# A hybrid trunk's layer: weights' sums in DRAM made later, rows' sums made in place block by block, and loads moved to GpSimd's queue

## The chip, the cores and the metric

The kernel runs on one core of a Trainium2 chip. The metric is device time in microseconds: the median of three executions. The trace is of one further execution, taken by the hardware profiler.

## The reference

One layer of a streaming encoder, float32, 1024 tokens (T) of width 1024 (D), and 256 memory tokens:

```python
h = layer_norm(a * x + stick_breaking(x @ sb_win) @ mix_wo)      # 16 heads of 64
h = layer_norm(a * h + cross_attention(h, mem) )                 # 4 heads of 256, with xa_wq, xa_wkv, xa_wo
u = h @ ffn_up                                                   # 1024 x 5632
u = causal_depthwise_conv(u, ffn_conv, width 3) + ffn_conv_b
g, val = split(u, 2)                                             # 2816 columns each
h = layer_norm(a * h + (gelu(g) * val) @ ffn_down)               # 2816 x 1024
```

with a = 2 ** 0.25; LayerNorm has a gain and a bias per column.

## The kernel before

**Products.** A float32 operand is split in two float32r parts, hi (a cast) and lo (the rest): `split` (lines 77 to 87). A product of two such operands is three matmuls, hi hi, hi lo, lo hi: `mm3` (lines 100 to 103). By default ScalarE casts (line 79) and VectorE subtracts (line 85); in some places GpSimd subtracts (line 87) or casts (line 83).

**Order.** The kernel is written in the program's order for a tile framework that assigns all semaphores. A planner with a simulated timeline then orders each engine's instructions: what is ready earlier in its simulation may go ahead of what is written earlier. An instruction in `keep_in_program_order` is not put ahead of the instruction written before it on its engine; others may pass it. Each engine, and each queue of DMAs (SyncE's, ScalarE's, GpSimd's), then works in that fixed order: a DMA that waits for a buffer holds those behind it. A tile of a pool with `reuse_waits="tile"` waits for the last use of just those older tiles whose memory it takes; `bufs` is the number of buffers that a tile name rotates through.

**Stages.** (1) Attention with all its projections; beside its end the memory's keys and values are made, and `wo` is split. (2) A loop of eight row blocks (`out_ln`, line 465): output projection (48 matmuls), residual, LayerNorm, transposes of the new rows. (3) Memory attention. (4) The same loop with the second LayerNorm; its rows go, transposed, into `h2f` (8 x 128 columns by 1024 rows) by `h2_evac`. (5) The MLP's first product (up), its convolution, GELU and gate, written to DRAM as `g_d`, 22 tiles of 128 x 1024. (6) The MLP's second product (down), the third LayerNorm, and the output.

**Both MLP products use seven products instead of eight on a 2 x 2 blocking (Strassen-Winograd).** They need sums of blocks of both factors.

*Up.* The rows' sums are t1 = b12 - b11, t2 = b22 - t1, t4 = b21 - t2 and t3 = b22 - b12, with b the four blocks of `h2f`. t3 is made in `h2_evac` per row block (line 596). The other three are made behind the loop, for k = 0 to 3, 12 subtractions of 128 x 512 (lines 707 to 713), each followed by its split. They take their memory from the three buffers `wt`, which are those of the weights' sums s1 to s4 (`Pair.sum`, line 630). The up weights come in 22 pairs of 128 columns; `Pair.block` (line 613) loads two blocks of 512 KB a pair (`wraw`, `wr`, two buffers each). Of the first two pairs the early products (`early1`, inside the last row block, and `early2`) run before the rows' sums are there, and `late` the rest. Then each step of the loop at line 792 runs `stage2` of a pair, `stage1` of the next, `stage3` of the pair. A pair ends in `gated`: convolution on ScalarE and VectorE, and for the second pair of two the gate product (line 739) and the store to `g_d` (line 740; on GpSimd's queue for the last pair).

*Down.* The weights' sums u1 to u4 are made in DRAM by DMAs alone (`u_steps`, line 419): 44 copies of 256 KB on SyncE's queue, then 44 DMAs on GpSimd's queue that add another block to what is there. They are interleaved in the two `out_ln` loops, six after the work of a block in the first loop, six ahead of a block in the second, as long as there are any. The down product runs seven products named m = 1, 6, 5, 7, 4, 3 and the last ("2", from line 945), each of 11 steps kt with four row blocks of 12 matmuls in all. A step loads a quarter of a gated tile (`slot(kt, s)`, 256 KB, line 824), a block of weights or of their sum (`w_block`, line 832, through pairs of `wraw`), splits both, and multiplies. Gated quarters are combined in place on VectorE (`plus`, line 854): in m = 1 slot 1 becomes slot 1 - slot 3 in the same step kt (line 905). The residual rows of h2 are loaded by `residual` (line 847) into two buffers `h2r` and added to an output quarter. In m = 4 a second weight block, "21", is loaded and split for the last product (line 917). The slots for kt under 5 are in the pool `ea`, the others in `ep`, behind the eight output rows `y`; both pools take memory that the MLP's first half had.

*End.* `finish` does the third LayerNorm of 128 rows and stores them. With `spread` it is shared: scale and bias on ScalarE, times the gain on GpSimd, plus the bias on VectorE, for each half of 512 columns (lines 452 to 456).

## Time and profile before

| | |
|---|---|
| time, median of 3 (lowest to highest) | 1591.94 us (1590.37 to 1593.48) |
| profiled execution: its time, its span | 1592.65 us, 1590.9 us |
| TensorE | 1521.3 us busy, 7508 matmuls |
| VectorE | 1100.6 us busy |
| ScalarE | 703.9 us busy |
| GpSimd | 643.4 us busy |
| mean granted TensorE clock | 0.981 of full speed |

The span goes from the first to the last instruction. PE is TensorE's matmuls, DVE VectorE, ACT ScalarE, POOL GpSimd, SPq SyncE's queue of DMAs; L85 is line 85. Matmuls overlap, so that a full stretch shows PE busy all the time, and the number of matmuls in it is the better measure. The granted clock is given in parts of 2.4 GHz; there are two levels, 1.00 and 0.50, so a value between them is a mean of both.

### The profile page before, as it was taken

How to read it: one execution, taken by the hardware profiler on the slowest of the kernel's cores; microseconds unless marked ns; L12 is line 12 of the kernel's file. 1: busy time of each engine (PE TensorE's matmuls, PEld its weight loads, DVE VectorE, ACT ScalarE, POOL GpSimd, SP SyncE). 2: the span in 40 equal slices, each digit the busy share in tenths (PEclk: the TensorE clock that was granted, in tenths of full speed). 3: DMA queues.
4: the chain of work that ended last, by engine and by line, in shares of the span. 5: the costliest groups of instructions: out<-in, count | busy, mean ns of one | idle time of the engine just before them, and what ended most of it. 6: DMA issues, size and time to landing. Idle time of an engine off the chain costs nothing.

```text
span 1590.9 us, 20977 instructions
## 1 busy us (share of the span) xinstructions
PE 1521.3 (96%) x7508; PEld 1267.0 (80%) x7508; DVE 1100.6 (69%) x1502; ACT 703.9 (44%) x1310; POOL 643.4 (40%) x571
## 2 busy tenths in 40 slices
PE   7999999999988999999999979999999999899897
PEld 5888888888877988788877757888888888688775
DVE  3366667667679646465445899877777777868795
ACT  4454555565566511133323244444444444344451
POOL 5775565565568800366405542323322231000033
PEclk9999999999999999999999989999999999899998
DMA  5322222221236548734449912222222224834531
GB/s 169 87 53 64 63 57 67 64 70 54 64 118 196 186 157 274 225 112 124 103 140 254 222 56 93 80 80 80 80 81 80 83 89 153 308 109 153 167 130 60
DMA packets 99192, 191.00 MB, mean 120 GB/s; under 512 B 11408, under 2 KB 33040, under 8 KB 99088
## 3 DMA queue, kind: packets, MB, share of 16 engines
q1 hardware_dynamic: 84400, 159.25, 31.5%
q0 software_dynamic: 6624, 12.59, 4.5%
q10 hardware_dynamic: 8064, 17.83, 3.2%
q8 instruction: 59, 0.97, 0.3%
q14 instruction: 45, 0.37, 0.1%
HBM read 146.63 MB, written 57.67 MB: 128 GB/s over the span
## 4 chain that ended last, share of the span: by engine, by line
PE 72%; DVE 10%; DMA 8%; POOL 4%; issue 4%; ACT 2%; SPq 1%; DVEq 0%; ACTq 0%; POOLq 0%
PE qkacc L101 4%; PE qkacc L103 3%; PE qkacc L102 3%; PE tp L231 3%; PE mb L101 3%; PE mb L103 3%; PE mb L102 3%; PE y L102 3%; PE y L103 3%; PE y L101 3%; PE ma L103 2%; PE ma L101 2%; PE ma L102 2%; PE mc L101 2%; PE mc L102 2%
## 5 line engine op out<-in xcount | busy, mean ns | idle before, releaser
L222 DVE TENSOR_TENSOR_SCAN sig<-sig 128x896 f32<-128x896 f32 (+7 forms) x128 | 196.8, 1544 | 73.9 <-POOL sig L219 55.2
L87 POOL TENSOR_TENSOR whl<-wraw,whl 128x512 fp32r<-128x512 f32 (+2 forms) x97 | 173.9, 1804 | 144.4 <-ACT whl L79 142.8
L448 POOL TENSOR_TENSOR rs<-rs,mhalf 128x1 f32<-128x1 f32 x24 | 23.7, 989 | 326.2 <-DVE rs L447 326.2
L85 DVE TENSOR_TENSOR wT<-tp,wT 128x512 fp32r<-128x512 f32 (+1 forms) x160 | 98.8, 629 | 62.4 <-ACT wT L79 61.2
L79 ACT CAST wT<-tp 128x512 fp32r<-128x512 f32 (+1 forms) x160 | 86.5, 545 | 103.9 <-PE tp L231 98.2
L79 ACT CAST whl<-wraw 128x512 fp32r<-128x512 f32 (+3 forms) x113 | 81.9, 738 | 97.6 <-PE y L103 34.5
L217 ACT ACTIVATE sig<-z 128x384 f32<-128x384 f32 (+2 forms) x192 | 92.1, 495 | 49.8 <-PE z L216 48.8
L101 PE MATMUL mb<-b_t,ws 128*128 128x512 f32 x264 | 105.0, 399 | 8.4 <-ACT ws L79 8.1
L101 PE MATMUL qkacc<-xh,whl 128*128 128x512 f32 x256 | 103.8, 405 | 7.6 <-ACT xh L79 6.2
L219 POOL TENSOR_SCALAR_AFFINE_SELECT sig<-sig 128x128 f32<-128x128 f32 x128 | 60.0, 472 | 119.5 <-ACT sig L217 113.6
L102 PE MATMUL y<-whl,aop 128*128 128x512 f32 x264 | 104.4, 397 | 1.6 <-DVE whl L85 1.6
L103 PE MATMUL mb<-b_t,ws 128*128 128x512 f32 x264 | 104.1, 396 | 0.0
L102 PE MATMUL mb<-b_t,ws 128*128 128x512 f32 x264 | 104.0, 394 | 0.0
L103 PE MATMUL qkacc<-xh,whl 128*128 128x512 f32 x256 | 101.9, 399 | 1.9 <-POOL whl L87 1.9
L102 PE MATMUL yacc<-wo,whl 128*128 128x512 f32 x256 | 102.4, 400 | 0.0
L102 PE MATMUL qkacc<-xl,whl 128*128 128x512 f32 x256 | 102.2, 399 | 0.0
L101 PE MATMUL yacc<-wo,whl 128*128 128x512 f32 x256 | 101.9, 398 | 0.2 <-ACT whl L79 0.2
L103 PE MATMUL y<-whl,aop 128*128 128x512 f32 x264 | 101.4, 396 | 0.0
L103 PE MATMUL yacc<-wo,whl 128*128 128x512 f32 x256 | 100.9, 396 | 0.0
L101 PE MATMUL y<-whl,aop 128*128 128x512 f32 x264 | 85.5, 398 | 12.3 <-ACT aop L79 7.6
L231 PE MATMUL tp<-ident,sig 128*128 128x128 f32 x576 | 89.4, 275 | 7.5 <-DVE wT L85 7.5
L79 ACT CAST ws<-wt 128x512 fp32r<-128x512 f32 x88 | 54.3, 620 | 95.5 <-PE mb L103 51.3
(214 smaller groups left out, 4355.6 us busy)
## 6 DMA issues: line engine op xcount, KB each, us to landing
u_d<-in_dn SPq DMA_DIRECT2D x44, 256.0 KB, 5.0
wraw<-in_up SPq DMA_DIRECT2D x22, 512.0 KB, 3.7
wr<-in_up SPq DMA_DIRECT2D x22, 512.0 KB, 3.6
float<-g_d SPq DMA_DIRECT2D x44, 256.0 KB, 5.6
wraw<-u_d SPq DMA_DIRECT2D x44, 256.0 KB, 2.9
g_d<-gate SPq DMA_DIRECT2D x20, 512.0 KB, 2.7
wraw<-in_dn SPq DMA_DIRECT2D x33, 256.0 KB, 3.0
q<-q SPq DMA_DIRECT2D x64, 128.0 KB, 2.2
```

The lines of the kernel that those rows point to most:

```text
L79: nc.scalar.copy(out=hi, in_=src)
L85: nc.vector.tensor_tensor(out=lo, in0=src, in1=hi.bitcast(F32), op=ALU.subtract)
L87: nc.gpsimd.tensor_tensor(out=lo, in0=src, in1=hi.bitcast(F32), op=ALU.subtract)
L101: nc.tensor.matmul(o, lhsT=lh, rhs=rh, start=first, stop=False, skip_group_check=more)
L102: nc.tensor.matmul(o, lhsT=lh, rhs=rl, start=False, stop=False, skip_group_check=more)
L103: nc.tensor.matmul(o, lhsT=ll, rhs=rh, start=False, stop=last, skip_group_check=more)
L217: nc.scalar.activation(out=sig[:, a:b], in_=z[:, :b - a], func=AF.Sigmoid, scale=-0.125)
L219: nc.gpsimd.affine_select(out=sig[:, S - P:S], in_=sig[:, S - P:S], pattern=[[-1, P]], base=-1, channel_multiplier=1, compare_op=ALU.is_ge ...
L222: nc.vector.tensor_tensor_scan(out=kr, data0=kr, data1=kr, initial=1.0, op0=ALU.mult, op1=ALU.bypass)
L231: nc.tensor.transpose(out=tp[:, k], in_=sigs[2 * d + u][:, P * j:P * j + P], identity=ident)
L448: nc.gpsimd.tensor_tensor(out=rs, in0=rs, in1=mhalf, op=ALU.pow)
```

## The change

- The generator of `u_steps` is made after the up product's first two pairs, and each step of the up loop takes five DMAs from it, ahead of `stage2`; both `out_ln` loops have none.
- t1, t2 and t4 are made in `h2_evac`, per row block of the second half, in `h2f` itself; behind the loop they are only split, t2 first.
- Gated quarters and the residual rows are loaded by GpSimd's queue; the residual rows have four buffers in `ep` instead of two in `ea`.
- In the down product the difference of m = 1 is made four steps later, the last four in m = 6; the weight block "21" of m = 4 has three buffers of its own.
- The LayerNorm of the very last row block is made without GpSimd's multiply: its first half by two operations on VectorE, its second by ScalarE and VectorE.

```diff
@@ -449,6 +449,15 @@
         if spread:
             nm = smallp.tile([P, 1], F32, name="nm")
             nc.vector.scalar_tensor_tensor(out=nm, in0=mv[:, 0:1], scalar=-1.0, in1=rs, op0=ALU.mult, op1=ALU.mult)
+            if spread == "last":
+                nc.scalar.activation(out=r[1], in_=r[1], func=AF.Identity, scale=rs, bias=nm)
+                nc.vector.scalar_tensor_tensor(out=r[0], in0=r[0], scalar=mv[:, 0:1], in1=g[:, 0:512],
+                                               op0=ALU.subtract, op1=ALU.mult)
+                nc.vector.scalar_tensor_tensor(out=r[0], in0=r[0], scalar=rs, in1=b[:, 0:512],
+                                               op0=ALU.mult, op1=ALU.add)
+                nc.vector.tensor_tensor(out=r[1], in0=r[1], in1=g[:, 512:], op=ALU.mult)
+                nc.vector.tensor_tensor(out=r[1], in0=r[1], in1=b[:, 512:], op=ALU.add)
+                return
             for c in range(2):
                 cs = slice(512 * c, 512 * c + 512)
                 nc.scalar.activation(out=r[c], in_=r[c], func=AF.Identity, scale=rs, bias=nm)
@@ -502,14 +511,11 @@
     def h1_evac(i, c, tp):
         split(tp, h1h[:, 4 * c:4 * c + 4, P * i:P * i + P], h1l[:, 4 * c:4 * c + 4, P * i:P * i + P])
 
-    u_sums = u_steps()
     with ExitStack() as c1:
         lnp = c1.enter_context(pool(name="ln1", bufs=1, side="right", reuse_waits="tile"))
         gb = load_ln(lnp, 0)
         for k, i in enumerate((4, 5, 2, 3, 0, 1, 6, 7)):
             out_ln(k, i, o_d, wts, xn, state["rp"], gb, h1_d, h1_evac)
-            for _ in range(6):
-                next(u_sums, None)
     mem_c.close()
 
 
@@ -593,9 +599,12 @@
         if th == 1 and c == 1:
             d = bs["t3"]
             t = lnp.tile([P, 4, P], F32, name="bt", bufs=2)
-            (nc.vector if i >= NTB - 2 else nc.gpsimd).tensor_tensor(
-                out=t, in0=h2f[:, 4:8, ts], in1=h2f[:, 0:4, ts], op=ALU.subtract)
+            b11, b21, b12, b22 = h2f[:, 0:4, cs], h2f[:, 4:8, cs], h2f[:, 0:4, ts], h2f[:, 4:8, ts]
+            (nc.vector if i >= NTB - 2 else nc.gpsimd).tensor_tensor(out=t, in0=b22, in1=b12, op=ALU.subtract)
             split(t, d[:, 0, :, cs], d[:, 1, :, cs])
+
+            for o, x, y in ((b11, b12, b11), (b12, b22, b11), (b21, b21, b12)):
+                nc.vector.tensor_tensor(out=o, in0=x, in1=y, op=ALU.subtract)
 
     e1c = ExitStack()
     e1 = {}
@@ -695,8 +704,6 @@
         rp = c3.enter_context(pool(name="rp2", bufs=2, reuse_waits="tile"))
         gb = load_ln(lnp, 1)
         for i in range(NTB):
-            for _ in range(6):
-                next(u_sums, None)
             out_ln(i, i, o2_d, wts2, h1_d, rp, gb, h2_d, h2_evac, first_products if i == NTB - 1 else None)
 
 
@@ -704,12 +711,9 @@
     bs.update({n: b3p.tile([P, 2, 4, 512], R, name=f"b_{n}") for n in ("t2", "t1", "t4")})
     for p in range(2):
         early2(pairs[p])
-    for k in range(4):
-        lo, hi = (slice(512 * th, 512 * th + 512) for th in range(2))
-        b11, b21, b12, b22 = h2f[:, k, lo], h2f[:, 4 + k, lo], h2f[:, k, hi], h2f[:, 4 + k, hi]
-        ts = [e1["a"].tile([P, 512], F32, name="wt", bufs=3) for _ in range(3)]
-        for t, n, x, y in ((ts[0], "t1", b12, b11), (ts[1], "t2", b22, ts[0]), (ts[2], "t4", b21, ts[1])):
-            nc.vector.tensor_tensor(out=t, in0=x, in1=y, op=ALU.subtract)
+    for n, k0, th in (("t2", 0, 1), ("t1", 0, 0), ("t4", 4, 0)):
+        for k in range(4):
+            t = h2f[:, k0 + k, 512 * th:512 * th + 512]
             split(t, bs[n][:, 0, k], bs[n][:, 1, k], "act", "pool" if n == "t4" else "dve")
     h2c.close()
     e1b = e1c.enter_context(pool(name="e1b", bufs=1, side="right", reuse_waits="tile"))
@@ -789,8 +793,11 @@
     late(pairs[1])
     pairs[2].factor("11", "s2", "s1")
     stage1(pairs[2])
+    u_sums = u_steps()
     for p in range(2, len(seq) - 1):
         w, nxt = pairs[p:p + 2]
+        for _ in range(5):
+            next(u_sums, None)
         stage2(w, nxt)
         if p + 1 < len(seq) - 1:
             nxt.factor("s2", "s1")
@@ -824,16 +831,19 @@
         def slot(kt, s):
             if (kt, s) not in slots:
                 t = slots[kt, s] = room(kt, s, F32)
-                nc.sync.dma_start(out=t, in_=g_d[NH * (s // 2) + kt][:, 512 * (s % 2):512 * (s % 2) + 512])
+                nc.gpsimd.dma_start(out=t, in_=g_d[NH * (s // 2) + kt][:, 512 * (s % 2):512 * (s % 2) + 512])
             return slots[kt, s]
 
         w_free = []
 
-        def w_block(n, kt):
-            if not w_free:
-                pair = wrawp.tile([P, 2, 512], F32, name="wraw")
-                w_free.extend((pair[:, 0], pair[:, 1]))
-            t = w_free.pop(0)
+        def w_block(n, kt, more=False):
+            if more:
+                t = ep.tile([P, 512], F32, name="wmore", bufs=3)
+            else:
+                if not w_free:
+                    pair = wrawp.tile([P, 2, 512], F32, name="wraw")
+                    w_free.extend((pair[:, 0], pair[:, 1]))
+                t = w_free.pop(0)
             nc.sync.dma_start(out=t, in_=u_d[n][kt] if n[0] == "u" else b_block(n, kt))
             return t
 
@@ -847,8 +857,8 @@
         def residual(n, b, x, op=ALU.add):
 
             i, ns = rows(n)[b]
-            t = ea.tile([P, 512], F32, name="h2r", bufs=2)
-            nc.sync.dma_start(out=t, in_=h2_d[i][:, ns])
+            t = ep.tile([P, 512], F32, name="h2r", bufs=4)
+            nc.gpsimd.dma_start(out=t, in_=h2_d[i][:, ns])
             nc.vector.scalar_tensor_tensor(out=quarters[n][b], in0=t, scalar=ALPHA, in1=x, op0=ALU.mult, op1=op)
 
         def plus(d, x, y, op=ALU.add):
@@ -895,14 +905,17 @@
                 s, u = plan[m]
                 x, t = slot(kt, s), ea.tile([P, 2, 512], R, name="aop", bufs=4)
                 if m == 6:
+                    if kt < 4:
+                        k7 = kt + NH - 4
+                        plus(slot(k7, 1), slot(k7, 1), slot(k7, 3), ALU.subtract)
                     plus(x, slot(kt, 1), x, ALU.subtract)
                 a, w = (t[:, 0], t[:, 1]), w_ops(kt)
                 split(x, *a)
                 split(w_block(u, kt), *w)
                 for b in range(4):
                     down(y[b], b, a, w, kt == 0 and not more, kt == NH - 1, more)
-                if m == 1:
-                    plus(slot(kt, 1), slot(kt, 1), slot(kt, 3), ALU.subtract)
+                if m == 1 and kt >= 4:
+                    plus(slot(kt - 4, 1), slot(kt - 4, 1), slot(kt - 4, 3), ALU.subtract)
                 elif m == 5:
                     nc.vector.scalar_tensor_tensor(out=slot(kt, 1), in0=slot(kt, 0), scalar=-1.0, in1=slot(kt, 3),
                                                    op0=ALU.mult, op1=ALU.subtract)
@@ -914,7 +927,7 @@
                         residual("11", kt - 7, c21[kt - 7])
                 elif m == 4:
                     last_ops[kt][1] = room(kt, 1, R), room(kt, 3, R)
-                    split(w_block("21", kt), *last_ops[kt][1])
+                    split(w_block("21", kt, True), *last_ops[kt][1])
                     if 3 <= kt < 7:
                         residual("21", kt - 3, c21[kt - 3])
                 elif m == 3:
@@ -948,7 +961,7 @@
                 down(y[b], b, *last_ops[kt], kt == 0, kt == NH - 1, False)
             plus(c11[b], c11[b], y[b])
             whole("11", b)
-            finish(b, True)
+            finish(b, "last" if b == 3 else True)
 
 
 def kernel(**inputs):
```

## Rows read from the trace of the kernel before

**Rows 1.** The page's busy time, share and instructions of each engine.
```profile
PE 1521.3 (96%) x7508; PEld 1267.0 (80%) x7508; DVE 1100.6 (69%) x1502; ACT 703.9 (44%) x1310; POOL 643.4 (40%) x571
```

**Rows 2.** Stretches: length, busy us (xinstructions) by engine, granted clock, DMA share, GB/s.
```profile
851.00:860.00 9.00, 6.75 (x27) 5.01 (x26) 8.25 (x16) 1.95 (x4) 5.95 (x7) 0.81 1.11 251
...
921.00:948.00 27.00, 17.61 (x67) 13.25 (x66) 24.58 (x37) 14.88 (x25) 8.07 (x6) 0.81 0.11 28
...
1000.00:1320.00 320.00, 320.00 (x1391) 260.77 (x1390) 242.86 (x282) 142.66 (x182) 94.33 (x52) 1.00 0.24 81
...
1364.00:1378.00 14.00, 6.58 (x18) 4.90 (x17) 7.46 (x9) 1.86 (x3) 0.84 (x2) 0.63 0.83 272
...
1378.00:1480.00 102.00, 102.00 (x452) 84.43 (x451) 79.96 (x129) 45.44 (x80) 0.00 (x0) 1.00 0.51 172
...
1480.00:1490.00 10.00, 5.26 (x16) 3.88 (x15) 8.07 (x15) 3.93 (x7) 0.00 (x0) 0.68 0.51 171
```

**Rows 3.** Timeline of PE: start, us, instructions, [idle before <-what ended it].
```profile
853.91 0.63 PE L493 MATMUL tp<-ident,r 128*128 128x128 f32 x4 [2.09 <-DVE r L462]
...
895.89 1.29 PE L493 MATMUL tp<-ident,r 128*128 128x128 f32 x8 [1.65 <-DVE r L462]
...
916.57 0.70 PE L493 MATMUL tp<-ident,r 128*128 128x128 f32 x4 [2.30 <-DVE r L462]
...
943.20 0.80 PE L101 MATMUL mb<-b_t,ws 128*128 128x512 f32 x1 [8.07 <-ACT ws L79]
...
1372.28 0.80 PE L101 MATMUL y<-whl,aop 128*128 128x512 f32 x1 [7.42 <-ACT aop L79]
...
1485.96 0.76 PE L101 MATMUL y<-whl,aop 128*128 128x512 f32 x1 [4.74 <-DVE y L855]
```

**Rows 4.** DMA issues in 840:900, 1000:1320 and 1466:1486: KB, median us to landing.
```profile
u_d<-u_d POOLq DMA_DIRECT2D x18, 256.0 KB, 12.4
...
r<-h_d ACTq DMA_DIRECT2D x10, 256.0 KB, 6.5
...
wr<-in_up SPq DMA_DIRECT2D x16, 512.0 KB, 3.5
...
g_d<-gate SPq DMA_DIRECT2D x16, 512.0 KB, 2.7
...
h2r<-h_d SPq DMA_DIRECT2D x7, 256.0 KB, 2.9
```

**Rows 5.** Timeline of POOL in the second LayerNorm loop.
```profile
887.22 5.04 POOL L426 DMA_DIRECT2D u_d<-u_d  x6
...
890.47 2.38 POOL L448 TENSOR_TENSOR rs<-rs,mhalf 128x1 f32<-128x1 f32 x1
```

**Rows 6.** DVE's groups by line in 900:950 and 1345:1364: busy, mean ns | idle.
```profile
L712 DVE TENSOR_TENSOR wt<-h2f,wt 128x512 f32<-128x512 f32 x8 | 6.9, 866 | 0.1
...
L855 DVE TENSOR_TENSOR float<-float,float 128x512 f32<-128x512 f32 x10 | 6.6, 683 | 0.0
```

**Rows 7.** Timeline of SPq and DVE in the up product.
```profile
1104.95 0.33 SPq L619 DMA_DIRECT2D wr<-in_up  x1
...
1116.29 0.69 DVE L631 TENSOR_TENSOR wt<-wr 128x512 f32<-128x512 f32 x1
```

**Rows 8.** Timeline of DVE, SPq and POOL at the turn to the down product.
```profile
1367.30 1.22 DVE L739 TENSOR_TENSOR gate<-gate,cv 128x1024 f32<-128x1024 f32 x1
...
1368.55 8.16 SPq L827 DMA_DIRECT2D float<-g_d  x13
...
1368.83 0.54 POOL L740 DMA_DIRECT2D g_d<-gate  x1 [4.53 <-DVE gate L739]
```

**Rows 9.** Timeline of SPq in the down product.
```profile
1472.93 4.99 SPq L851 DMA_DIRECT2D h2r<-h_d  x3
```

**Rows 10.** The chain that ended last, in order of time: start, us, what.
```profile
1582.07 0.56 POOL rs L448
...
1585.04 1.73 DVE y L456
```

## The prediction

> **What bounds the kernel now.** I read the page's busy times first: TensorE is busy 96% of the span and no other engine over 69% [rows 1]. So the time is TensorE's work plus the places where it waits, and the question is which of these places the change reaches. Next I read the stretches: the reader is to compare the number of matmuls with the length. In the MLP's steady products 1391 start in 320 us, 4.35 per us, at a granted clock of 1.00; in the down product 452 in 102 us, 4.43 per us. Against these paces three stretches fall short, and what is missing, divided by the pace, is the time lost there [rows 2]:
> - 921 to 948: 67 of 117 matmuls, 27 - 67/4.35 = 11.6 us.
> - 1364 to 1378: 18 of 62, 14 - 18/4.43 = 9.9 us.
> - 1480 to 1490: 16 of 44, 10 - 16/4.43 = 6.4 us.
>
> Part of each loss comes after the wait itself: the granted clock in these stretches is 0.81, 0.63 and 0.68 on average, so a part of each runs at the lower level, 1.2 GHz, after TensorE has stood. Last I read TensorE's own rows for who ended each wait: 8.07 us <- ScalarE's cast of a weights' sum, 7.42 us <- the cast of a gated block, 4.74 us <- VectorE, and in the second LayerNorm loop 2.09, 1.65 and 2.30 us <- VectorE's last LayerNorm step [rows 3].
>
> The profiled execution took 1592.65 us, 1.75 us more than its span and 0.71 us above the median of the three timed runs (1591.94). I sum against 1592.65 and take off 0.71 at the end.
>
> **Part 1, weights' sums out of the LayerNorm loops.** The 44 copies and 44 accumulating DMAs leave both loops. In 840 to 900 us 18 accumulating DMAs of one form run; they land after 12.4 us in the median, and a residual row of 256 KB beside them after 6.5 us, where a 256 KB row lands in 2.9 us late in the kernel [rows 4]. The wait at 853.91 follows such a late row: 2.09 us of standing and, in 851 to 860, a clock of 0.81, which is (1 - 0.81) x 9 = 1.7 us more [rows 2, 3]. Together 3.8, bounds 0 and 3.8; I take 2.8, since something can still be late by a little. The wait at 895.89 is GpSimd's: six accumulating issues hold it from 887.22 for 5.04 us, and the LayerNorm's power is stretched among them to 2.38 us (0.56 where nothing is near, at the end of the chain) [rows 5, 10]. That 1.65 us goes.
>
> Where they go: 5 per pair of up-product tiles, 18 iterations of 19.3 us each (7 products of 12 matmuls, 84/4.35). A weight block is loaded a pair ahead: issued at 1104.95, it lands 3.5 us later and VectorE first reads it at 1116.29, so it has 11.3 - 3.5 = 7.8 us to spare [rows 4, 7]. No trace shows the sums beside these loads. Nearest rows: a load beside the accumulating DMAs landed 3.6 us later than alone (6.5 against 2.9), inside the 7.8; the accumulating DMA itself took 12.4. GpSimd's issues, 5 x 0.84 = 4.2 us (5.04 for six), stand in front of GpSimd's next split; SP's five copies in front of the next weight load. Both are covered as long as less than 7.8 us is added. I take 1 us of loss in all; lower end 0 (nothing in this stretch is waiting now, so no gain), upper end 18 x (12.4 + 3.5 - 11.3) = 83 us, were every weight block as late as an accumulating DMA. I take the value near the first row because a plain load is what waits here, not an accumulation.
>
> **Part 2, sums of rows in place.** Before, 12 subtractions (L712, 0.87 us mean, some stretched) stand between the last row block and the first "late" product, interleaved with their splits, and the weights' sums of the first pair share their three buffers and queue behind them; that is the 8.07 us wait [rows 3, 6]. After, 9 of the 12 are done in earlier blocks, and 3 of 0.69 us remain behind the last one; the sums no longer share buffers. VectorE's work from the last transposes (921) to the first late product is then 3 pieces of t3 and b22 (2.1), 3 subtractions (2.1), 8 splits (5.5), sums and splits of the pair (3.4) and two combinations (1.3): 14.4 us, against 24 + 24 matmuls of early products, 11 us, and the first late product needs only the first half of it. So the wait goes save about 1.5 us: gain 10; bounds 4.8 (VectorE late by the whole 14.4 - 11 = 3.4, and as much again by the clock) and 11.6. The price: in the last four blocks VectorE gets 3 x 0.69 = 2.1 us more each, and in the last the wait of 2.30 us at 916.57 is already open [rows 3]. I charge 2.1 there, which eats the 1.65 of part 1; bounds 0 and 4 with the clock.
>
> **Part 3, gated rows by GpSimd's queue; deferred differences.** At the turn to the down product TensorE has the first five blocks' products and then waits for the sixth gated block. Its load is issued at 1368.55, right as the last gate product ends (1367.30 + 1.22) [rows 8]: its buffer lies on the convolution's scratch tile. That follows from the tile sizes too, counted in KiB of a partition from where these pools begin: 20 slots (40), operands (16), two h2r tiles (4) and lo2 (2) make 62, the eight output rows 32, so the slot lies at 94 to 96. From the other side, 182.6 less 38 for the weights' pool and 48 for the rows' sums leaves 96.6; the last 4 below it are the convolution's scratch, the 4 below those the second gate tile. With h2r's 4 gone from its pool the slot, still the first behind the output rows, lies at 90 to 92, on that gate tile, whose last reader is not VectorE but the store of it. So the load waits for the store to land: issue 0.54 [rows 8], landing 2.7 [rows 4], and its own issue on GpSimd is about 0.2 us longer than on SP (0.54 against 0.33, SP's of 1104.95 [rows 7]): 3.4 us later. (The Trainium skill, DMA: Bandwidth & Descriptors, Specifications, gives a first byte of about 1 us on GpSimd's path and 0.6 on SP's; no run here isolates that. By an estimate from this page the term is 0.4 us worse and the sum 0.4 lower.) Against it: 10 differences of 0.683 us stand in VectorE's queue in 1345 to 1364, among the last convolutions [rows 6]; the change defers five of them by four blocks. If half of them leave, the last gate ends 5 x 0.68 = 3.4 us earlier; I take 1.4, since the planner can put others there. Net loss 2; bounds -7 (nothing leaves, and the slow clock costs as much again as the 3.4) and +5 (all ten leave the last gate's way, 6.8, and the clock gains with it).
>
> **Part 4, residual rows on GpSimd's queue, weights of the second set in their own tiles.** The 4.74 us wait ends with VectorE's difference on the bank that the next product adds to. VectorE had stood behind residual rows, and ScalarE behind a weight block that SP issued late: three residual loads with two buffers hold SP from 1472.93 for 4.99 us, though one lands in 2.9 [rows 4, 9]. With the loads on another queue and four buffers SP only meets weights. Gain 5.5 of 6.4; bounds 0 and 6.4. (The Trainium skill, DMA: Bandwidth & Descriptors, Issuing engines are not separate DMA queues, says that issuing from several engines saves only the issue time, since all run on the same 16 DMA engines. By that rule nothing is gained here and the sum is 5.5 lower; it is a rival below. The trace speaks for the queue: it is held by waits for buffers, not by transfers.)
>
> **Part 5, last row block.** The chain's end: GpSimd's power at 1582.07 + 0.56, ScalarE, GpSimd's multiply, then VectorE's add from 1585.04, stretched to 1.73, and a second one of 0.6, to 1587.4 [rows 10]. After: four VectorE operations of 0.69 from the moment the scale and its product are there (1582.6 + 0.2), ending at 1585.6, with ScalarE beside the first two. Gain 1.8, bounds 1.5 (each 0.08 longer) and 2.4 (the first runs before the power).
>
> Sum: 2.8 + 1.65 - 2.1 + 10 - 2 + 5.5 + 1.8 - 1 = 16.65 us. 1592.65 - 16.65 = 1576.0; less 0.71: 1575.3 us.
>
> **Rivals.**
> - The turn gets shorter as well (part 3 at +5, parts 1, 2 and 4 at their full 3.8, 11.6, 6.4): 16.65 + 7 + 3.5 = 27.15 us, 1564.8. For it: VectorE is full in that stretch, and every difference gone counts. Against: the gate's store.
> - VectorE takes over from the wait at 943, as its 24.58 busy us in 27 say [rows 2]: part 2 gives 4.8 instead of 10, and the turn is at -7: 16.65 - 5.2 - 5 = 6.45, 1585.5. Against: 8 us of its work there are moved ahead.
> - A different queue saves only issue time: part 4 gives nothing, 11.15 us, 1580.8. For it: the moved bytes are the same, 0.51 of the DMA engines' time in 1480 to 1490 [rows 2]. Against: SP's row [rows 9]. This is also the way in which the change doesn't do what it says.
> - Slower: the sums in DRAM make weight blocks late. Place: VectorE's first sum of each pair, 18 times. It decides once a block lands more than 11.3 us after its issue; the whole gain is gone at 16.65/18 = 0.9 us more, 12.2 us, about an accumulating DMA's median [rows 4]. At 13 us: 18 x 1.7 = 30.6 us, against 17.65 of the other parts, 1604.9. For it: these DMAs fill the engines in 840 to 900. Against: there six came per row block of 11 us (48 matmuls at 4.4 per us) and here five per 19.3, and the DMA share of the up product is 0.24 now [rows 2].
>
> **Chances.** Forecast (gain 9 to 24) 0.55; shorter turn 0.13; VectorE takes over 0.12; issue time only 0.08; weight blocks late 0.09 (of it 0.02 within 0.2%); the rest 0.03, no change that shows. The measurement tells 0.2%, 3.2 us, from no change. Faster: 0.55 + 0.13 + 0.12 + 0.08 = 0.88; slower 0.07; same 0.05. Range: from 1563, past the shorter turn, to 1589, past VectorE's rival; about 0.2 lies outside. Forecast alone: 1568 to 1583.
>
> **What would show it.** In the profile after: no L426 rows before 1000; the LayerNorm power rows (L448) in the second loop near 1 us; no wait over 3 us and a clock of 1.00 between 920 and 950 (step 2); the wait at the turn 6 to 12 us, ended by a load issued after the gate's store landed (step 3); no wait of 4 us where the fourth product of the down part follows on the same banks (step 4); the last output issued 4 us after the last row's statistics (step 5). Wrong if TensorE's pace in the up product falls under 4.35 per us, or if the wait near 943 stays over 4 us.

## The result, and the profile after

The changed kernel takes 1571.19 us (median of four runs, 1568.83 to 1574.44) against 1591.15 us for the kernel before on the same chip (1585.77 to 1593.48): ratio 0.9881, 95% interval 0.9849 to 0.9912. Predicted were 1575.3 us, from 1563 to 1589. Its profiled execution took 1570.6 us with a span of 1568.8 us, so the spans differ by 22.1 us.

I place these 22.1 us first by the starts of a few matmuls that both kernels have, before looking at waits. The lengths of five stages, in us, and in the last column the gain that the prediction's terms give for the stage:

| stage | before | after | gain | predicted |
|---|---|---|---|---|
| start to the first output projection (code unchanged) | 561.3 | 559.2 | 2.1 | 0 |
| A: first LayerNorm loop and memory attention, to the last `o2acc` | 251.3 | 247.6 | 3.7 | 0 |
| B: second LayerNorm loop, to the last `yacc` | 92.6 | 83.2 | 9.4 | 2.8 + 1.65 |
| C: last row block and up product, to the last `mc` | 439.7 | 431.7 | 8.0 | 10 - 2.1 - 1 |
| D: down product, to the last `y` | 234.9 | 237.0 | -2.1 | 5.5 - 2 |
| E: from there to the end | 11.2 | 10.1 | 1.0 | 1.8 |

The first line is a measure of chance: nothing is changed there (and stage A came out 1.9 us shorter and 1.4 longer in two kernels below that are unchanged in it). So the sum came out near the forecast because two terms were too small by 8.7 us together (A, B) and one stage lost where it should have gained (D), 5.6 us the other way: that these two nearly cancel is luck.

The page's busy times after (answering to [rows 1]):

```profile
PE 1508.8 (96%) x7508; PEld 1261.5 (80%) x7508; DVE 1086.4 (69%) x1504; ACT 701.5 (45%) x1309; POOL 676.8 (43%) x629
```

Stretches of the changed kernel; the columns are those of [rows 2]. In order: the second LayerNorm loop, the last row block, the steady up product, the turn to the down product, the steady down product, and the place of the old wait ahead of the fourth product:

```profile
838.00:847.00 9.00, 9.00 (x45) 7.44 (x44) 8.46 (x16) 3.62 (x7) 0.99 (x1) 1.00 0.42 149
903.00:913.00 10.00, 5.68 (x17) 3.72 (x18) 8.81 (x16) 3.72 (x8) 2.92 (x1) 0.66 0.30 105
980.00:1300.00 320.00, 320.00 (x1391) 260.77 (x1390) 242.50 (x282) 143.42 (x182) 131.96 (x96) 1.00 0.53 140
1337.00:1364.00 27.00, 10.76 (x36) 8.32 (x35) 12.04 (x17) 5.53 (x9) 9.35 (x18) 0.68 0.67 234
1364.00:1466.00 102.00, 102.00 (x452) 84.42 (x451) 81.64 (x132) 45.39 (x81) 13.57 (x25) 1.00 0.51 175
1464.00:1474.00 10.00, 9.01 (x41) 7.17 (x40) 7.70 (x13) 4.80 (x9) 0.00 (x0) 1.00 0.28 85
```

The loop runs at full clock with TensorE busy throughout. The up product has 1391 matmuls in 320 us, exactly as before, though the DMA share there went from 0.24 to 0.53. Two stretches stand out: 903 to 913 and, much worse, 1337 to 1364, with 36 matmuls in 27 us. TensorE's waits there (answering to [rows 3]):

```profile
905.78 0.61 PE L101 MATMUL mc<-b,ws 128*128 128x512 f32 x1 [1.32 <-ACT b L79]
908.16 0.80 PE L101 MATMUL mc<-b,ws 128*128 128x512 f32 x1 [1.78 <-ACT ws L79]
909.97 1.22 PE L101 MATMUL mb<-b_t,ws 128*128 128x512 f32 x2 [1.01 <-ACT b_t L79]
...
1357.66 0.80 PE L101 MATMUL y<-whl,aop 128*128 128x512 f32 x1 [16.24 <-ACT aop L79]
...
1467.74 0.47 PE L101 MATMUL y<-whl,aop 128*128 128x512 f32 x1 [0.99 <-DVE y L865]
```

The wait of 8.07 us at the first late product is gone, that of 4.74 us is down to 0.99, and that of 7.42 us at the turn has become 16.24. GpSimd's rows at the turn, then SyncE's queue beside them (answering to [rows 8]):

```profile
1345.80 0.53 POOL L744 DMA_DIRECT2D g_d<-gate  x1 [7.32 <-DVE gate L743]
1354.01 5.98 POOL L834 DMA_DIRECT2D float<-g_d  x11 [7.67 <-DMA g_d<-gate]
```

```profile
1343.92 0.43 SPq L435 DMA_DIRECT2D lng<-in_lng  x1
1344.40 0.43 SPq L436 DMA_DIRECT2D lnb<-in_lnb  x1
1344.87 2.48 SPq L847 DMA_DIRECT2D wmore<-in_dn  x3
```

The sixth gated block's load does wait for the landing of the last gate's store, as the prediction had it from the addresses. But the store does not land in 2.7 us: it takes 7.4 (1345.80 + 0.53 to 1353.72). Five loads left SyncE's queue around it (four in the 1.9 us before it, the fifth with it), and the trace of before has them elsewhere: there the gated quarters stood in that queue, and the third LayerNorm's gain and bias went out behind them, at 1380.86.

### The profile page after: what moved, and what is told of

Read it like the earlier page. It is cut to its first block, busy times and chain, and to the rows that moved or that the text cites. A ratio compares the mean times of both kernels' runs of the same rounds, so it can differ in the third digit from the quotient of the medians.

```text
span 1568.8 us, 21007 instructions
## 1 busy us (share of the span) xinstructions
PE 1508.8 (96%) x7508; PEld 1261.5 (80%) x7508; DVE 1086.4 (69%) x1504; ACT 701.5 (45%) x1309; POOL 676.8 (43%) x629
## 4 chain that ended last, share of the span: by engine, by line
PE 82%; DVE 5%; POOL 5%; issue 4%; DMA 2%; ACT 1%; SPq 0%; POOLq 0%; DVEq 0%; ACTq 0%
PE yacc L101 4%; PE yacc L102 4%; PE yacc L103 4%; PE qkacc L101 4%; PE qkacc L103 4%; PE qkacc L102 4%; PE tp L231 3%; PE mb L101 3%; PE mb L103 3%; PE mb L102 3%; PE y L102 3%; PE y L103 3%; PE y L101 3%; PE mc L102 2%; PE mc L101 2%
## 5 line engine op out<-in xcount | busy, mean ns | idle before, releaser
L222 DVE TENSOR_TENSOR_SCAN sig<-sig 128x896 f32<-128x896 f32 (+7 forms) x128 | 193.0, 1514 | 76.8 <-POOL sig L219 57.9
L101 PE MATMUL yacc<-wo,whl 128*128 128x512 f32 x256 | 100.5, 393 | 0.4 <-ACT whl L79 0.4
L103 PE MATMUL yacc<-wo,whl 128*128 128x512 f32 x256 | 100.8, 394 | 0.0
L102 PE MATMUL yacc<-wo,whl 128*128 128x512 f32 x256 | 100.7, 393 | 0.0
```

The costliest lines, as they stand in the source:

```text
L101: nc.tensor.matmul(o, lhsT=lh, rhs=rh, start=first, stop=False, skip_group_check=more)
L102: nc.tensor.matmul(o, lhsT=lh, rhs=rl, start=False, stop=False, skip_group_check=more)
L103: nc.tensor.matmul(o, lhsT=ll, rhs=rh, start=False, stop=last, skip_group_check=more)
L222: nc.vector.tensor_tensor_scan(out=kr, data0=kr, data1=kr, initial=1.0, op0=ALU.mult, op1=ALU.bypass)
```

## The experiments

Each kernel was timed beside runs of the kernel before on the same chip. Where a stage is compared, it is one of the table's.

**Each part alone.** `p1only` is the kernel before with the sums' DMAs moved:

```diff
-            for _ in range(6):
-                next(u_sums, None)      # in both LayerNorm loops
...
+    u_sums = u_steps()
...
+        for _ in range(5):
+            next(u_sums, None)          # in the up product's loop
```

> The kernel before with the first part alone: the weights' sums in DRAM are made in the up product, five DMAs a step, and nothing else is changed. Theory A (the sums' DMAs stand in the way of both what VectorE reads and what GpSimd does in the second LayerNorm loop, and cost more there than the two waits that the prediction counted): the output projection's last matmul comes 7 to 12 us earlier than before, the wait of 8.07 us at the first product with t2 stays, the up product keeps its pace of 4.35 matmuls per us, and the time is 7 to 12 us under before, about 1582. Rival B (the prediction's sizes): 3.5 us, 1588. Rival C (most of what the whole change gained ahead of the up product belongs to the rows' sums in place, which let the planner put work elsewhere): under 2 us, 1590.

Measured: 1578.27 us, ratio 0.9920 (0.9907 to 0.9932), some 12.7 us. Stages A and B are 247.7 and 83.2 us, the changed kernel's to 0.1 us; C is 0.6 us longer than before, and the wait at the first product with t2 is still 8.20 us. Theory A holds, a little beyond its numbers (7 to 12 us, about 1582); the sizes of the prediction (B) do not. In the second LayerNorm loop the residual rows land 3.0 us after their issue (median), where the kernel before has 6.9, and TensorE does not stand at all, where before it was busy for 87.83 of 92.20 us (812.9 to 905.1) at a granted clock of 0.98. Sixty microseconds of the second loop before, and the same place in `p1only`:

```profile
840.00:900.00 60.00, 56.03 (x255) 45.10 (x254) 38.66 (x66) 15.36 (x27) 25.94 (x29) 0.97 1.04 246
```

```profile
827.00:887.00 60.00, 60.00 (x288) 49.73 (x287) 44.38 (x73) 18.60 (x33) 10.30 (x9) 1.00 0.40 138
```

The DMA engines go from full to 0.40. A part of the gain is order, not waiting: in the planned sequence of TensorE's instructions 48 matmuls of the second output projection, and not 40, stand ahead of the last `o2acc`. Eight matmuls are 1.8 us that leave B; and in A they fill the place where the kernel before waits at 805 us. Its rows there, and the one that `p1only` has:

```profile
805.37 0.41 PE L560 MATMUL tpp<-ident,p 128*128 128x128 f32 x2 [1.44 <-DVE p L557]
806.21 0.41 PE L560 MATMUL tpp<-ident,p 128*128 128x128 f32 x2 [0.44 <-DVE p L557]
807.08 0.73 PE L101 MATMUL o2acc<-pT,vh 128*128 128x512 f32 x2 [0.46 <-ACT pT L79]
```

```profile
801.86 0.51 PE L101 MATMUL yacc<-wo,whl 128*128 128x512 f32 x1 [0.43 <-ACT whl L79]
```

`p2only` is the kernel before with the rows' sums in place:

```diff
+            for o, x, y in ((b11, b12, b11), (b12, b22, b11), (b21, b21, b12)):
+                nc.vector.tensor_tensor(out=o, in0=x, in1=y, op=ALU.subtract)   # in h2_evac
...
-        for t, n, x, y in ((ts[0], "t1", b12, b11), (ts[1], "t2", b22, ts[0]), (ts[2], "t4", b21, ts[1])):
-            nc.vector.tensor_tensor(out=t, in0=x, in1=y, op=ALU.subtract)       # behind the loop
```

> The kernel before with the second part alone: t1, t2 and t4 are made in place in the row blocks of the second half. Theory A (the wait at the first product with t2 goes, and a part of it comes back in the last row block, where VectorE has three more subtractions ahead of the splits that the early products read): the stretch from the last output projection to the first product with t2 is 5 to 7 us shorter, 1584 to 1587. Rival B (the prediction's sum, 10 less 2.1): 1583. Rival C (without the first part the LayerNorm loop is late by the sums' DMAs anyway, so the three subtractions cost nothing and the whole 11.6 us are gained): 1579 to 1580.

Measured: 1585.06 us, ratio 0.9958 (0.9945 to 0.9971). Stage C is 7.1 us shorter, B 1.0 us longer. Theory A, with 6.1 us over both stages; and the prediction's 7.9 is not far off. What came back stands in the last row block, which was to be the price; where the kernel before waits 1.32 us for the same cast, it is now:

```profile
923.74 1.22 PE L101 MATMUL mc<-b,ws 128*128 128x512 f32 x2 [4.23 <-ACT b L79]
```

`downonly` is the kernel before with the down product's loads, buffers and deferred differences, without the new last LayerNorm:

```diff
-                nc.sync.dma_start(out=t, in_=g_d[...])
+                nc.gpsimd.dma_start(out=t, in_=g_d[...])
...
-            t = ea.tile([P, 512], F32, name="h2r", bufs=2)
-            nc.sync.dma_start(out=t, in_=h2_d[i][:, ns])
+            t = ep.tile([P, 512], F32, name="h2r", bufs=4)
+            nc.gpsimd.dma_start(out=t, in_=h2_d[i][:, ns])
```

> The kernel before with the third and fourth part alone: gated and residual rows loaded by GpSimd's queue, four buffers for residual rows behind the output rows, the differences of m = 1 deferred, the block 21 of m = 4 in buffers of its own; the last LayerNorm stays as before. Theory A (the residual rows' buffers leave the first pool, so the sixth gated quarter comes to lie on the second gate tile, and its load waits for the landing of that tile's store): TensorE's wait at the turn grows from 7.42 us to 14 to 18 us, the wait of 4.74 us later in the down product goes, and the time is 1 to 4 us over before, 1592 to 1595. Rival B (the long turn of the changed kernel comes from what stands ahead of it, not from this part): the wait at the turn stays 6 to 9 us and the time falls by 4 to 6 us, 1585 to 1587.

Measured: 1596.52 us, ratio 1.0031 (1.0020 to 1.0043): slower, by 3 to 7 us. Its wait at the turn:

```profile
1383.46 0.79 PE L101 MATMUL y<-whl,aop 128*128 128x512 f32 x1 [18.32 <-ACT aop L79]
```

Theory A, a little beyond its numbers at both. Stage D is 2.8 us longer than before. Another 2.1 us lie between the last output's landing and the end of the span; the trace shows nothing there, and I leave them open.

**What the turn waits for.** `early` places the quarters (5,0) to (10,0) ahead of the output rows, the first four of them on memory that is free early:

```diff
+        slots, first = {}, {kt: room(kt, 0, F32) for kt in range(5, NH)}
         rs = [ep.tile([P, D], F32, name=f"y{i}") for i in range(NTB)]
...
+                t = slots[kt, s] = first[kt] if kt > 4 and s == 0 else room(kt, s, F32)
```

> The changed kernel, with one thing moved: the buffers of the gated quarters (5,0) to (10,0) are placed ahead of the eight output rows and not behind them, so that the first four of them lie on memory that held t3 and rows of h2, free long before the last gate. Theory A (the wait at the turn, 16.4 us in the changed kernel, is for memory, and there are six more steps of 2.7 us of work for TensorE once the quarters have it): the wait falls under 3 us, no stretch at the lower clock follows it, and the time is 12 to 17 us under the changed kernel's 1571, 1554 to 1559. Rival B (ScalarE and VectorE are full with the last convolutions at the turn, so the casts and rests of the quarters come no earlier): TensorE still waits 8 us or more in all, and the time is 1563 to 1568. Rival C (GpSimd's queue itself is late, since each of its quarters' loads comes behind the gate's store): the wait stays as it is, 1570.

Measured: 1568.26 us, ratio 0.9858 (0.9844 to 0.9871). The wait is 14.57 us and no longer 16.24. My theory A, that memory alone makes the wait, fell; rival C was right on the cause, though the wait is 1.67 us shorter and not as it was:

```profile
1344.45 0.53 POOL L744 DMA_DIRECT2D g_d<-gate  x1 [7.32 <-DVE gate L743]
1344.97 3.79 POOL L832 DMA_DIRECT2D float<-g_d  x7
```

The load now waits for no landing, but it stands behind the store on the same queue, and the store waits 7.32 us for VectorE's gate. It then landed only at 1353.60, 8.1 us after its issue, beside the same five loads. My reading is that the planner did not put it ahead of the store because the second pool as a whole overlaps the last gates; no run shows the planner's reason. `moved` puts all eleven quarters (kt,0) in the first pool, which does not overlap them, and the (kt,2), wanted last, in the second:

```diff
-            return (ea if kt < 5 else ep).tile(
+            return (ea if s == 0 or kt < 5 and s != 2 else ep).tile(
```

> The changed kernel, with the gated quarters shared out otherwise over the two pools: all eleven quarters (kt,0) lie in the first pool, whose memory is free before the last gates, and the quarters (kt,2), which are wanted last, go behind the output rows. All eleven loads then stand ahead of the stores of the last two gates on GpSimd's queue; in the run with the quarters ahead of the output rows they still stood behind them, and TensorE waited 14.6 us. Theory A (the turn is a matter of which load stands behind which store on GpSimd's queue): TensorE runs through all eleven steps of the first product, 29 us from 1325, the wait at the turn falls under 4 us, and the time is 11 to 16 us under the changed kernel's 1571, 1555 to 1560. Rival B (the loads that now stand behind the stores are those of the second product, and VectorE's deferred differences wait for them): a wait of 8 us or more stands at the start of the second product, some 1354, and the time is 1564 to 1569.

Measured: 1552.90 us (1550.72 to 1554.78), ratio 0.9759 (0.9742 to 0.9776), the fastest version here. GpSimd's rows, and TensorE from the first matmul of the down product:

```profile
1330.14 4.61 POOL L834 DMA_DIRECT2D float<-g_d  x7 [0.46 <-DMA float<-g_d]
1339.50 0.54 POOL L744 DMA_DIRECT2D g_d<-gate  x1 [4.74 <-DVE gate L743]
1351.46 0.53 POOL L744 DMA_DIRECT2D g_d<-gate  x1 [11.42 <-DVE gate L743]
1361.79 3.79 POOL L834 DMA_DIRECT2D float<-g_d  x7 [9.80 <-DMA wmore<-in_dn]
```

```profile
1326.00:1356.00 30.00, 30.00 (x134) 24.78 (x133) 26.72 (x39) 13.13 (x21) 7.26 (x14) 1.00 0.67 231
```

The last seven of the early loads go out by 1334.75, ahead of both stores; no wait of 1 us is left in the turn, and stage D is 219.5 us, 17.5 less than in the changed kernel. Theory A, with a little more than its numbers: the wait is one of places in a queue, and it is shown. The last store lands no sooner than in the changed kernel (9.5 us after its issue); now TensorE does not wait for it.

`slot_sp` takes the other way: the changed kernel with the quarters on SyncE's queue again, ahead of the five loads.

```diff
-                nc.gpsimd.dma_start(out=t, in_=g_d[...])
+                nc.sync.dma_start(out=t, in_=g_d[...])
```

> The changed kernel with the gated quarters loaded by SP's queue again; their buffers stay where the change puts them, (5,0) on the second gate tile. On SP's queue the quarters stand ahead of the third LayerNorm's gain and bias and of the three blocks 21, five loads that in the changed kernel, where SP had no quarters to load, went out just ahead of the last gate's store. Theory A (of the 16.4 us at the turn the buffer costs the landing of the store and of the load, some 3 us each, and the rest is those five loads beside the store, which landed after 7.39 us and not after 2.7): the store lands in 3 to 5 us, the wait at the turn is 10 to 13 us, 1564 to 1568. Rival B (the buffer alone; what goes out beside the store is nothing): the wait stays at 15 to 17 us, 1570 to 1573. Rival C (the quarters belong on GpSimd's queue for the whole down product, SP's weights are late otherwise): more waits later, 1573 or more.

Measured: 1569.94 us, ratio 0.9869 (0.9853 to 0.9886). The wait is 14.35 us, between A and B. The store lands in 2.4 us, as A had it. But GpSimd's queue, now without quarters, sent four residual rows early, and they took the place of the five loads:

```profile
1347.55 0.54 POOL L744 DMA_DIRECT2D g_d<-gate  x1 [4.54 <-DVE gate L743]
1348.09 2.15 POOL L861 DMA_DIRECT2D h2r<-h_d  x4
```

The quarter, issued at 1350.56, lands after 5.5 us, not 2.3. `nomore`, the changed kernel with the blocks "21" back in the weights' buffers, takes three of the five away:

```diff
-                    split(w_block("21", kt, True), *last_ops[kt][1])
+                    split(w_block("21", kt), *last_ops[kt][1])
```

> The changed kernel with the blocks 21 loaded through the weights' buffers again, as before; the residual rows keep GpSimd's queue and four buffers. Theory A (the residual rows' buffers alone end the wait; and at the turn two large loads and no longer five go out just ahead of the last gate's store): no wait over 1.5 us between the third and the fourth product; the store of the last gate lands 1 to 3 us sooner than 7.39 us, the wait at the turn is 13.5 to 15.5 us, and the time is 1568 to 1571. Rival B (the blocks 21 hold the weights): 4 to 6 us of waits in the second half of the down product, 1574 or more.

Measured: 1569.79 us, ratio 0.9864 (0.9841 to 0.9887). The store lands in 6.5 us and the wait is 15.66, just short of A's range: the gain and bias, 512 KB each, weigh more than the three blocks, which cost the store under 2 us (in `sums22` below, whose turn is the changed kernel's, it takes 8.1 us and the wait is 16.4). No wait over 1.5 us stands ahead of the fourth product.

**The residual rows.** `h2r_sp` is the changed kernel with these loads on SyncE's queue, with four buffers; `h2r_sp2` has two buffers as well.

```diff
-            t = ep.tile([P, 512], F32, name="h2r", bufs=4)
-            nc.gpsimd.dma_start(out=t, in_=h2_d[i][:, ns])
+            t = ep.tile([P, 512], F32, name="h2r", bufs=4)      # h2r_sp2: bufs=2
+            nc.sync.dma_start(out=t, in_=h2_d[i][:, ns])
```

> The changed kernel with the residual rows of the down product loaded by SP's queue again, with their four buffers. Theory A (the wait of 4.74 us in the kernel before came from two buffers for the rows, which held SP, and not from the queue; this is also what the rule that a queue saves only issue time would give): no wait over 1.5 us between the third and the fourth product, the time within 2 us of the changed kernel's, 1569 to 1573. Rival B (weights and rows on one queue keep each other late): a wait of 3 to 5 us with a stretch at the lower clock comes back, 1575 to 1578.

> The changed kernel with the residual rows on SP's queue and with two buffers, as before, while the blocks 21 keep their own three. Theory A (what held SP in the kernel before was a residual load waiting for its buffer, three of them from 1472.93 for 4.99 us, with the weights behind it): TensorE's wait of 4 to 6 us ahead of the fourth product comes back, with a stretch at the lower clock, and the time is 1575 to 1578. Rival B (the wait went because the blocks 21 no longer share the weights' buffers): no wait over 1.5 us there, 1570 to 1573.

Measured: 1571.76 us, ratio 0.9879 (0.9862 to 0.9895), and 1575.56 us, ratio 0.9905 (0.9885 to 0.9926). Ahead of the fourth product, first with four and then with two buffers:

```profile
1470.45 0.47 PE L101 MATMUL y<-whl,aop 128*128 128x512 f32 x1 [0.48 <-DVE y L865]
```

```profile
1472.55 0.47 PE L101 MATMUL y<-whl,aop 128*128 128x512 f32 x1 [3.03 <-DVE y L865]
```

and SyncE's queue with two, three loads held as in [rows 9]:

```profile
1455.27 4.03 SPq L861 DMA_DIRECT2D h2r<-h_d  x3
1459.58 0.79 SPq L847 DMA_DIRECT2D wraw<-u_d  x2
1461.39 4.15 SPq L861 DMA_DIRECT2D h2r<-h_d  x3
```

So on SyncE's queue two more buffers remove the wait, and the other queue was not needed. Whether GpSimd's queue with two buffers would do it as well, no run shows. (The Trainium skill, DMA: Bandwidth & Descriptors, Issuing engines are not separate DMA queues, has it that another issuing engine saves only issue time: by `h2r_sp`, 1571.76 against 1571.19 us, this case agrees for the rows.) The wait that came back is 3.03 us with no lower clock after it, less than theory A's 4 to 6.

**The DMAs of the sums.** `acc_plain` is the kernel before with the accumulations made plain copies, which leaves the additions out.

```diff
-                    accum_op=ALU.add, max_dma_last_dim=2048))
+                    max_dma_last_dim=2048))
```

> The kernel before with the 44 accumulating DMAs of the weights' sums made plain copies, on the same queue at the same places (the additions are left out, so the down product has other weights). Theory A (the accumulations fill the DMA engines, and the residual rows, projection weights and keys behind them land late): the DMA share of the second LayerNorm loop falls from 1.00 to under 0.8, the last output projection matmul comes 8 to 12 us earlier, and the time is 1580 to 1584. Rival B (GpSimd is held by issuing 44 DMAs of 0.84 us among the LayerNorms' steps, whatever they do): nothing but the 2 to 3 us of late rows goes, 1588 to 1591.

Measured: 1586.95 us, ratio 0.9973 (0.9961 to 0.9984). The DMA share of 840 to 900 falls from 1.04 to 0.70, but stage B is 92.8 us, as before, and rows still land late: issued at 838.63, one lands after 9.3 us, beside copies that take 10.0 and 10.4, and TensorE waits for VectorE, which waits for such rows:

```profile
849.09 0.51 PE L101 MATMUL yacc<-wo,whl 128*128 128x512 f32 x1 [1.77 <-DVE r L486]
852.80 1.08 PE L493 MATMUL tp<-ident,r 128*128 128x128 f32 x4 [2.27 <-DVE r L462]
```

The time lies between the two theories: A falls in its size, and B in its reason. Two rows of GpSimd's groups, in 650 to 910, before and then here:

```profile
L426 POOL DMA_DIRECT2D u_d<-u_d x22 | 18.4, 1263 | 3.5 <-DMA u_d<-u_d 2.6 <-DMA u_d<-in_dn 0.8
```

```profile
L426 POOL DMA_DIRECT2D u_d<-u_d x22 | 11.6, 534 | 0.0
```

The issues got shorter too, and the loop did not. So neither the addition nor the length of GpSimd's issues is what costs the loop. What is left are the 256 KB transfers in front of the rows, added or copied (the rows land after 6.9 us in the median of the loop before, 5.0 here, 3.0 in `p1only`), and the order that the planner makes around them; these runs do not part the two.

`sums22` makes four steps of the up product carry all the sums:

```diff
-        for _ in range(5):
+        for _ in range(22):
```

> The changed kernel with 22 DMAs of the weights' sums in each of four steps of the up product, and not five in each of eighteen. Theory A (a weight block has 7.8 us to spare, and a plain load beside the accumulations is late by less than that): the up product keeps 4.35 matmuls per us, and the time is within 3 us of the changed kernel's 1571. Rival B (the mechanism of the slower case: once the DMA engines are full, each weight block is late by 1.7 us or more, and SP's eleven or more copies and GpSimd's issues of 0.84 us stand in front of the next pair's load and split): TensorE waits 2 to 8 us in each of the four steps, 1579 to 1603.

Measured: 1591.76 us, ratio 1.0004 (0.9991 to 1.0016): the whole gain is gone. Stage C is 454.3 us, 22.6 more:

```profile
940.00:980.00 40.00, 36.60 (x151) 28.71 (x149) 29.11 (x33) 15.55 (x20) 6.52 (x4) 0.96 1.01 331
980.00:1060.00 80.00, 69.37 (x269) 54.19 (x270) 54.70 (x55) 29.64 (x38) 55.83 (x55) 0.89 0.86 180
1060.00:1300.00 240.00, 240.00 (x1042) 195.47 (x1042) 187.26 (x215) 105.39 (x135) 70.54 (x39) 1.00 0.29 93
```

Rival B, so the slower case's mechanism exists: with the DMA engines full, VectorE waits for a weight block; beside it TensorE's waits of 2.80 and 2.37 us end, at 982.16 and 985.75:

```profile
982.34 2.76 DVE L640 TENSOR_TENSOR wt<-wr 128x512 f32<-128x512 f32 x1 [3.81 <-DMA wr<-in_up]
```

The block landed 9.3 us after its issue, less than the prediction's 11.3, but it was issued late as well, behind the step's copies on SyncE's queue. GpSimd is busy 55.83 of 80 us with these issues and its own work, and what that adds is not parted from the blocks. The pace is back once the sums are through. Five a step stay under that: there the blocks land after 3.6 us in the median, against 3.5 before.

**The last row block.** `moved_pool` is `moved` with GpSimd making the last block's three subtractions.

```diff
-                nc.vector.tensor_tensor(out=o, in0=x, in1=y, op=ALU.subtract)
+                (nc.gpsimd if i == NTB - 1 else nc.vector).tensor_tensor(out=o, in0=x, in1=y, op=ALU.subtract)
```

> The version with all eleven quarters (kt,0) in the first pool, and beside it the three subtractions for t1, t2 and t4 of the last row block made by GpSimd, not by VectorE. Theory A (VectorE, full from the last rows to the first product with t2, is what the waits of 1.5, 2.2 and 1.6 us there go back to, so 3 operations of 0.68 us less are worth 2 us or, with the clock, 4): 1549 to 1551. Rival B (GpSimd takes 1.3 us or more for each and slows VectorE beside it, and t2's casts then wait for GpSimd): 1553 to 1556.

Measured: 1553.01 us, ratio 0.9763 (0.9748 to 0.9777), against 1552.90 and 0.9759: no gain, rival B. Stage C is 1.5 us longer than in `moved`; the times are equal only because stage D, where nothing was changed, came out 2.0 us shorter. GpSimd's first subtraction takes 1.25 us (the other two 3.27 together), and VectorE's operation beside it 1.74 where the next takes 0.69:

```profile
906.08 1.74 DVE L640 TENSOR_TENSOR wt<-wt,wraw 128x512 f32<-128x512 f32 x1 [1.16 <-POOL ws L87]
907.85 0.69 DVE L640 TENSOR_TENSOR wt<-wraw,wt 128x512 f32<-128x512 f32 x1
```

(The Trainium skill, SBUF — State Buffer, SBUF: two separate sides, says that GpSimd and a VectorE operation with two SBUF inputs lock each other out for a whole instruction. These rows agree.)

## Why the prediction was right, and where its steps were off

**Part 1, the sums out of the loops: predicted 2.8 + 1.65 - 1, measured about 13 (`p1only`).** Both waits went as said, and the loss of 1 in the steady up product did not come. The step that failed is "Together 3.8, bounds 0 and 3.8; I take 2.8", with the two waits as all that the sums cost. Without the eight moved matmuls stage B gained 7.6 us where 2.8 + 1.65 were said: 255 matmuls stood in the 60 us of [rows 4], 288 do now, and (288 - 255)/4.35 is 7.6. Some 6 of these 7.6 us are TensorE's standing in the whole loop (92.20 - 87.83) and the lower clock (0.02 x 92.20). The 3.7 us of A and 1.8 of B I did not look for: with 88 DMAs fewer the planner orders TensorE's work otherwise.

**Part 2: predicted 10 - 2.1, measured 8.0 in stage C, with no loss in the up product.** Mechanism and size hold. The price fell where it was put, in the last row block: the wait of 2.30 us ahead of its transposes is gone, but 1.78 and 1.01 us stand behind them that were not there before, with a granted clock of 0.66 in 903 to 913. VectorE is busy 8.81 of these 10 us.

**Part 3, the turn: predicted -2, measured -8.8** (93 matmuls in the first 40 us of the down product and not 132, at 4.43 per us), beyond the bound of -7. The buffer was right: the load waits for the landing of the store (the 182.6 KiB behind the address stand in no trace). The wait itself is 16.24 us, outside the sign of 6 to 12. Two terms failed. The larger is the store's landing, "2.7": that row is of stores in the up product, at a DMA share of 0.24. Here it is 7.4, and the granted clock of 0.68 in that stretch adds to the loss; in the kernel before this very store, beside gated quarters, already took 5.1 (issued by 1369.37, landed at 1374.45). The other is the gain of 1.4 from deferred differences: it did not come. Counted from the last matmul into `mc`, where stage D begins, the last gate ends after 23.7 us before and 23.8 after, and in 1321.7 to 1345.5, ahead of its end, ten differences stand as they do in [rows 6]:

```profile
L865 DVE TENSOR_TENSOR float<-float,float 128x512 f32<-128x512 f32 x10 | 6.5, 681 | 0.0
```

The planner put others there, which the prediction had named as a reason to take only 1.4. The load is issued 8.5 us after the gate's end and no longer with it, which is nearly all of what the wait grew by (8.8). No run defers the differences alone. The prediction asked what the moved loads meet on GpSimd's queue, and not what leaves SyncE's queue once they are gone from it. And the whole wait was avoidable, by `moved`.

**Part 4: predicted 5.5, measured 5.6** (84 matmuls in 20 us around the place and not 59). With part 3 this makes -3.2 for stage D; 1.1 us come back elsewhere in it. The mechanism is half right: four buffers do it without the queue (`h2r_sp`), and the blocks' own buffers were not needed (`nomore`). The rival "issue time only" was right on the queue and wrong on the time.

**Part 5: predicted 1.8, measured 1.8 in the work, 1.0 in stage E.** From the last matmul to the issue of the last output it is 7.69 us before and 5.86 after:

```profile
1579.72 0.39 PE L103 MATMUL y<-float32r,float32r 128*128 128x512 f32 x1
...
1587.41 0.34 ACTq L870 DMA_DIRECT2D out_dram<-y  x1
```

```profile
1558.69 0.39 PE L103 MATMUL y<-float32r,float32r 128*128 128x512 f32 x1
...
1564.55 0.34 ACTq L880 DMA_DIRECT2D out_dram<-y  x1
```

The rest lies behind that: the last output lands 2.0 to 2.1 us after this issue in both, and the span ends 1.4 us later before and 2.3 after (1.0 in `h2r_sp`, with the same end of the program); the trace shows nothing there. The way to the 1.8 was not quite the one forecast. The power was taken at 0.56, from a row with nothing beside it; after, VectorE's first step runs beside it, not behind it, and it takes 0.99:

```profile
1560.88 0.74 DVE L454 SCALAR_TENSOR_TENSOR y<-y,mv,lng 128x512 f32<-128x512 f32 x1
1561.04 0.99 POOL L448 TENSOR_TENSOR rs<-rs,mhalf 128x1 f32<-128x1 f32 x1 [3.02 <-DVE rs L447]
```

**The rivals.** The slower one did not come at five DMAs a step, and `sums22` shows it at 22. "VectorE takes over" came in part, in the last row block alone. The shorter turn was wrong in sign.

## What to carry to other kernels

When a group of loads leaves a queue, list what stood behind it there: it goes out earlier, and lands beside whatever is urgent at that moment. Before the price of a transfer is taken from a row, see what else was in flight in that row. And where a stage begins with loads on the same queue as the stores that end the stage before, give those loads memory that the planner can see free before the stores.

## What the runs showed of the hardware

- A 512 KB store landed in 2.4 us with nothing else in flight when it was issued (`slot_sp`), 5.1 beside 256 KB loads (the kernel before), 6.5 beside two 512 KB loads (`nomore`), and beside these and three of 256 KB in 7.4 (the changed kernel) to 9.5 us (`moved`).
- A 512 KB weight load landed after 3.5 us (median) at a DMA share of 0.24 and after 3.6 at 0.53 (up product, before and after).
- Accumulating DMAs and plain copies of 256 KB left the second LayerNorm loop equally long (92.6 and 92.8 us), though the accumulations take more of the DMA engines (1.04 against 0.70 in 840 to 900).
- GpSimd's one-column power took 0.56 us alone and 0.99 beside a VectorE operation.
